# Attention inside a hybrid decoder block: q's and k's split parts made for two heads at once and copied into place, and v's shifted rows loaded into the value tile

## The chip, the cores and the metric

The kernel runs on one core of one Trainium2 chip. The metric is the device time of one execution in microseconds (us); what is given is the median of several runs. One execution was also recorded by the hardware profiler, and all rows of the profile come from it.

The engines carry short names: PE is TensorE (matrix products; PEld is its weight load), DVE is VectorE, ACT is ScalarE, POOL is GpSimd, SP is SyncE, which here issues nearly all DMA transfers. Each engine works through its own queue of instructions in order. L852 is line 852 of the kernel.

## The reference

One layer of a decoder: parallel token mixing (stick-breaking attention with 16 heads of 64, a state-space mixer and two gates), cross-attention into 256 memory tokens, and a gated feed-forward part, each between two norms. The sequence has 1024 tokens, the model 1024 channels, in float32. The change touches the stick-breaking attention only:

```python
z = jnp.einsum('bhtd,bhsd->bhts', qf[:, :, t0:t1], kf[:, :, :t1])   # qf is q / sqrt(64)
causal = jnp.arange(t1)[None, :] < (t0 + jnp.arange(SB_BLOCK))[:, None]
log_1mb = jnp.where(causal, jax.nn.log_sigmoid(-z), 0.0)
tail = lax.cumsum(log_1mb, axis=3, reverse=True)
w = jnp.where(causal, jnp.exp(z + tail), 0.0)
outs.append(jnp.einsum('bhts,bhsd->bhtd', w, vf[:, :, :t1]))
```

A weight is the chance of breaking the stick at position s times the chance of not having broken it between s and t. With N(s) the product of (1 - sigmoid) from s to t, the weight is N(s+1) - N(s), so the sum over s of weight times v can be written with N and with differences of neighbouring rows of v.

## The kernel before

All products are done on PE with each float32 operand split into a high part that PE's format holds and the low rest: hi x hi, hi x lo and lo x hi are added up in PSUM (`mm3`, L101). So every operand needs two instructions on its way: a copy that rounds (mostly on ACT) and a subtraction that gives the rest (mostly on DVE).

The kernel has these stages: projections with the two-level scheme `winograd_pair`, the attention, the state-space mixer, cross-attention and the feed-forward part. The attention is the loop over `m` from L927: a unit is one head and one half (512) of its queries, four units are a pair of heads. While one unit's values are formed, the scores of the next unit and pieces of a projection are interleaved with it (`interleave`, L903).

For each unit:
- `scores` (L837): for each block of 128 queries, two matmuls per 512 keys (L849, L850) with q's tile `qs` as the weights and `kh`, `kl` as the moving operand; ACT takes the sigmoid of the negative (L851), and DVE runs a product scan backwards over the row (L852). The head has 64 channels and PE has 128 rows, so the rows 0 to 63 of `qs` hold the high part of q and the rows 64 to 127 the low part; `kh` holds k's high part in both halves of its rows, `kl` the low part in both. One matmul then gives two of the products.
- `values` (L859): PE transposes the scanned blocks (L868), ACT makes the high part of N - 1 (`wth`, L871), DVE the low part (`wtl`, L872), and two matmuls add them to the head's output with the value tile `v` as the weights (L880, L881). The output's two halves of rows are added by ACT and DVE (L888, L889) and go to memory as `oT`.
- `differences` (L822): for an even head, v's rows and the rows shifted by one are loaded for both heads (`va`, `vb`, L828, one buffer each), POOL subtracts them (L829), and for each head POOL writes the high and low part into the value tile `v` (L833, L834; two buffers, one per head of the pair).

The projections of q and k for a pair of heads are run two pairs ahead (`qk_proj`, L782; `qk_quanta`, L911): `dense` (L758) loads 128 columns of the weights, splits them into `whi` and `wlo`, and forms each half of the result (128 rows, 64 per head) by 24 matmuls into one of two PSUM buffers. When a half is done, it is evacuated: `ev_q` (L786) or `ev_k` (L797). For each head a copy over its 64 rows goes to ACT and a subtraction over 64 rows to DVE; for k, two DMAs then copy rows 0 to 63 of `kh` and `kl` to rows 64 to 127 (L808, L809). `qs`, `kh` and `kl` have four buffers, so those of two pairs.

The order of each engine's instructions is not the program's order: the framework simulates the program with priced instructions, takes what is ready by priority, and lays that order down, with semaphores for what depends on another engine. `issue_behind` (L212) ties a projection's matmuls behind the eighth last marked attention matmul (L772). A tile's buffer is reused only when all that reads the tile before it is done.

Of the kernel before, what the change touches and what calls it, by code (L numbers as in the profile page):

```python
# [16 lines left out]
P = 128  # L17
# [3 lines left out]
NCH = S // P  # L21
HALF = 512
# [3 lines left out]
NH, HD = 16, 64  # L26
# [9 lines left out]
def hybrid_block(ctx, tc, a, out, dbg=None):  # L36
    nc = tc.nc
    V, A, G, T = nc.vector, nc.scalar, nc.gpsimd, nc.tensor

    def pool(stack, name, bufs=1, space=None, side=None):  # L40
        kw = {} if space is None else {"space": space}
        if side is not None:
            kw["side"] = side
        if space is not DRAM:
            kw["reuse_waits"] = "tile"
        return stack.enter_context(tc.tile_pool(name=name, bufs=bufs, **kw))
# [40 lines left out]
    def hi_sb(o, i, eng=None):  # L87
        if eng is None:
            turn[0] += 1
            eng = "pa"[turn[0] % 2]  # L90
        if eng == "p":
            G.tensor_scalar(o, i, 1.0, 0.0, ALU.mult, ALU.add)  # L92
        elif eng == "v":
            V.tensor_copy(o, i)
        else:
            A.activation(o, i, AF.Copy)  # L96

    def lo_of(o, i, hi, eng=V):
        eng.tensor_tensor(o, i, hi.bitcast(F32), ALU.subtract)  # L99
# [151 lines left out]
    with ExitStack() as pa:  # L251
# [382 lines left out]
        with ExitStack() as p1:  # L634
# [4 lines left out]
            t2 = pool(p1, "t2c", 2)  # L639
# [96 lines left out]
        with ExitStack() as p2:  # L736
            wp = pool(p2, "w2", 2, side="right")
            vp = pool(p2, "vp", 2, side="right")
            t2 = pool(p2, "t2b", 2, side="right")
# [18 lines left out]
            def dense(c0, evac):  # L758

                st = {}  # L760

                def first():
                    st["w"] = load_split(wp, colblock(w_in, c0), [P, KT, P], 1)

                def part(half, kk):
                    def run():
                        if kk == 0:
                            st["ps"] = mk(psm, [P, HALF], F32, "mm")
                        whi, wlo = st["w"]
# [12 lines left out]
            def qk_proj(hp):  # L782
                for j in range(2):
                    heads[2 * hp + j] = {}

                def ev_q(ps, half):  # L786
                    sl = slice(half * HALF, (half + 1) * HALF)
                    for j in range(2):
                        hd = heads[2 * hp + j]
                        if half == 0:  # L790
                            hd["q"] = mk(qk, [P, S], F32R, "qs")
                        pj = ps[j * HD:(j + 1) * HD]
                        q = hd["q"]
                        A.activation(q[0:HD, sl], pj, AF.Copy)
                        V.tensor_tensor(q[HD:P, sl], pj, q[0:HD, sl].bitcast(F32), ALU.subtract)

                def ev_k(ps, half):  # L797
                    sl = slice(half * HALF, (half + 1) * HALF)
                    for j in range(2):
                        hd = heads[2 * hp + j]  # L800
                        if half == 0:
                            hd["kh"] = mk(qk, [P, S], F32R, "kh")
                            hd["kl"] = mk(qk, [P, S], F32R, "kl")
                        pj = ps[j * HD:(j + 1) * HD]
                        kh, kl = hd["kh"], hd["kl"]
                        A.activation(kh[0:HD, sl], pj, AF.Copy)
                        V.tensor_tensor(kl[0:HD, sl], pj, kh[0:HD, sl].bitcast(F32), ALU.subtract)
                        nc.sync.dma_start(kh[HD:P, sl].bitcast(F32), kh[0:HD, sl].bitcast(F32))  # L808
                        nc.sync.dma_start(kl[HD:P, sl].bitcast(F32), kl[0:HD, sl].bitcast(F32))  # L809

                return dense(C_Q + hp * P, ev_q), dense(C_K + hp * P, ev_k)

# [9 lines left out]
            def differences(h):  # L822

                j = h % 2
                if j == 0:
                    va, vb = [mk(vp, [P, NCH, P], F32, n, bufs=1) for n in ("va", "vb")]
                    for t, r in ((va, 0), (vb, 1)):
                        nc.sync.dma_start(t, v_d[r:S + r, h * HD:(h + 2) * HD].rearrange("(c p) d -> p c d", p=P))  # L828
                    G.tensor_tensor(va, va, vb, ALU.subtract)  # L829
                    dvs[0] = va  # L830
                dv = dvs[0][:, :, j * HD:(j + 1) * HD]
                vt = mk(vp, [P, NCH, P], F32R, "v")
                hi_sb(vt[:, :, 0:HD], dv, "p")  # L833
                lo_of(vt[:, :, HD:P], dv, vt[:, :, 0:HD], G)  # L834
                heads[h]["v"] = vt
# [91 lines left out]
            for m in range(NM):  # L927
                h, half = m // 2, m % 2
                hp, r = m // 4, m % 4
# [4 lines left out]
                if m >= NM - 5:  # L934
                    n = -(-len(late) // (NM - m))
# [10 lines left out]
    with ExitStack() as p3:  # L946
# [4 lines left out]
        t2 = pool(p3, "s2p", 9)  # L951
# [4 lines left out]
        ps = pool(p3, "ps3", 1, PSUM)  # L956
# [347 lines left out]
    with ExitStack() as p4:  # L1304
# [3 lines left out]
        t2 = pool(p4, "t2m", 4)  # L1308
        ps = pool(p4, "ps4", 4, PSUM)
# [20 lines left out]
        for f in range(KT):  # L1330
# [3 lines left out]
            for half in range(2):  # L1334
                sl = slice(half * HALF, (half + 1) * HALF)
# [77 lines left out]
    with ExitStack() as q1:  # L1413
# [19 lines left out]
    with ExitStack() as q2:  # L1433
# [68 lines left out]
        for m in range(2):  # L1502
            t = mk(t4, [P, D], F32, "x4")
# [36 lines left out]
    with ExitStack() as q4:  # L1540
# [3 lines left out]
        t2 = pool(q4, "t2f", 6, side="right")  # L1544
# [333 lines left out]
```

## Time and profile before

| | |
|---|---|
| Median of 3 runs | 2579.89 us (2579.11 to 2581.29) |
| Profiled execution: time, and span of the records | 2581.7 us, 2580.0 us |
| Attention: first score matmul, last value matmul | 668.3 us, 1091.1 us |
| Distance at which a pair of heads repeats | 49.66 us |
| Granted PE clock between 660 and 1080 us | 1.00 |
| SP issues for k's copies (L808 and L809) | 32 and 32, 128 KB each |

The profile page gives for each engine its busy time and share of the span. Other views of the same execution are used: a table of windows (busy time of every engine in each stretch, granted clock, share of the DMA engines, GB/s), a list of waits (which line of which engine stood for which other, in total, times and longest), and the timeline (start, length, engine, line, output and inputs; in square brackets the idle time of the engine before it and what ended it). Lengths given as three numbers are minimum, median and maximum in ns.

### The profile page before, as it was taken

What the parts mean: (1) busy time and instruction counts of PE and PEld (TensorE: products, weight loads), DVE (VectorE), ACT (ScalarE), POOL (GpSimd) and SP (SyncE); (2) the same over time, 40 slices, a digit from 0 to 9 for tenths busy, and PEclk for the clock granted to TensorE, in tenths of its full rate; (3) what the DMA queues carried; (4) which work ended last, traced back from release to release, by engine and by line L of the source; (5) the groups of instructions that cost most, each with busy time, mean ns of one, the idle gap of its engine ahead of it and who ended that gap; (6) DMA issues with size and microseconds to landing.
All of it is one profiled execution on the core that took longest, in us unless ns stands there. A gap on an engine that the chain in (4) does not pass through costs nothing.

```text
span 2580.0 us, 32652 instructions
## 1 busy us (share of the span) xinstructions
PE 2488.6 (96%) x12026; PEld 2061.7 (80%) x12026; DVE 1819.7 (71%) x2119; ACT 1148.6 (45%) x2052; POOL 882.8 (34%) x690
## 2 busy tenths in 40 slices
PE   8999999999999999979999999999999999999998
PEld 6788787887788788767888788887787888887776
DVE  7685777766688898677888554416459666666997
ACT  6343455555466665556545312314333333334433
POOL 5331554443121121135655231101114323323675
PEclk9999999999999999989999999999999999999999
DMA  6441443334322322355332452311232232234322
GB/s 230 148 154 61 131 135 98 100 108 129 98 78 58 89 69 68 98 164 184 115 92 72 154 165 94 129 51 49 88 113 73 78 96 76 79 95 170 131 98 98
DMA packets 244331, 278.54 MB, mean 108 GB/s; under 512 B 15039, under 2 KB 171848, under 8 KB 243786
## 3 DMA queue, kind: packets, MB, share of 16 engines
q1 hardware_dynamic: 244170, 276.45, 33.7%
q8 instruction: 95, 1.56, 0.2%
q14 instruction: 66, 0.54, 0.1%
HBM read 197.87 MB, written 70.13 MB: 104 GB/s over the span
## 4 chain that ended last, share of the span: by engine, by line
PE 73%; DVE 12%; DMA 6%; issue 4%; ACT 3%; POOL 2%; SPq 0%; POOLq 0%; DVEq 0%; ACTq 0%
PE mm L220 8%; PE mm L222 8%; PE mm L221 8%; PE mm L102 7%; PE mm L104 7%; PE mm L103 7%; PE tr L868 2%; PE p L102 2%; PE p L103 2%; PE p L104 2%; DVE op L99 2%; PE pd L1090 2%; DVE n L852 2%; PE av L881 1%; PE ma L294 1%
## 5 line engine op out<-in xcount | busy, mean ns | idle before, releaser
L852 DVE TENSOR_TENSOR_SCAN n<-n,mask 128x128 f32<-128x128 f32 (+7 forms) x128 | 176.4, 1403 | 11.0 <-ACT n L851 10.3
L99 DVE TENSOR_TENSOR sw<-sf,sw 128x512 fp32r<-128x512 f32 x150 | 129.1, 873 | 66.2 <-ACT sw L96 65.7
L196 POOL TENSOR_TENSOR sf<-wr,wr 128x512 f32<-128x512 f32 x38 | 59.1, 1555 | 287.2 <-DMA wr<-in_w_gu_dram 138.7
L871 ACT ACTIVATE wth<-tr,mone 128x512 fp32r<-128x512 f32 x192 | 110.9, 580 | 73.3 <-PE tr L868 71.7
L96 ACT ACTIVATE sw<-sf 128x512 fp32r<-128x512 f32 x150 | 91.8, 626 | 99.2 <-PE mm L222 84.5
L99 DVE TENSOR_TENSOR sw<-wr,sw 128x512 fp32r<-128x512 f32 x113 | 110.3, 979 | 32.8 <-ACT sw L96 32.8
L872 DVE SCALAR_TENSOR_TENSOR wtl<-tr,wth 128x512 fp32r<-128x512 f32 x192 | 101.6, 546 | 39.9 <-ACT wth L871 38.5
L222 PE MATMUL mm<-h,sw 128*128 128x512 f32 x320 | 124.8, 391 | 1.8 <-DVE sw L99 1.8
L96 ACT ACTIVATE sw<-wr 128x512 fp32r<-128x512 f32 x113 | 70.8, 629 | 124.1 <-PE mm L222 123.9
L220 PE MATMUL mm<-h,sw 128*128 128x512 f32 x320 | 122.6, 391 | 3.1 <-ACT h L96 2.3
L221 PE MATMUL mm<-h,sw 128*128 128x512 f32 x320 | 125.1, 391 | 0.0
L102 PE MATMUL mm<-oth,bw 128*128 128x512 f32 (+1 forms) x320 | 122.4, 382 | 2.5 <-DVE a L1149 2.2
L104 PE MATMUL mm<-oth,bw 128*128 128x512 f32 (+1 forms) x320 | 119.5, 373 | 0.8 <-DVE bw L1136 0.5
L103 PE MATMUL mm<-otl,bw 128*128 128x512 f32 (+1 forms) x320 | 118.9, 371 | 0.0
L92 POOL TENSOR_SCALAR v<-va 128x512 fp32r<-128x512 f32 x16 | 21.0, 1316 | 272.5 <-PE av L881 147.9
L667 DVE SCALAR_TENSOR_TENSOR b<-b,prmT,b 128x1023 f32<-128x1023 f32 (+2 forms) x72 | 106.5, 1481 | 9.9 <-ACT b L665 9.4
L851 ACT ACTIVATE n<-sc 128x512 f32<-128x512 f32 (+1 forms) x192 | 89.0, 486 | 50.4 <-PE sc L850 26.5
L165 POOL TENSOR_SCALAR rstd<-ms 128x1 f32<-128x1 f32 x82 | 27.7, 338 | 239.4 <-ACT x L1370 102.5
L102 PE MATMUL p<-bw,h 128*128 128x512 f32 x256 | 99.5, 394 | 3.3 <-DVE x L1372 2.4
L104 PE MATMUL p<-bw,h 128*128 128x512 f32 x256 | 100.6, 394 | 0.0
L103 PE MATMUL p<-bw,h 128*128 128x512 f32 x256 | 100.5, 393 | 0.0
L198 POOL TENSOR_TENSOR sf<-wr 128x512 f32<-128x512 f32 x38 | 63.2, 1663 | 108.2 <-DVE sw L99 108.2
(592 smaller groups left out, 8171.5 us busy)
## 6 DMA issues: line engine op xcount, KB each, us to landing
wr<-in_w_gu_dram SPq DMA_DIRECT2D x80, 256.0 KB
wr<-in_w_in_dram SPq DMA_DIRECT2D x36, 512.0 KB
zr<-in_w_in_dram SPq DMA_DIRECT2D x32, 512.0 KB
gu_d<-t SPq DMA_DIRECT2D x44, 256.0 KB
wraw<-in_w_in_dram SPq DMA_DIRECT2D x20, 512.0 KB
xs_d<-b SPq DMA_DIRECT2D x32, 256.0 KB
s<-xs_d SPq DMA_DIRECT2D x32, 256.0 KB
s<-zs_d SPq DMA_DIRECT2D x32, 256.0 KB
```

The costliest lines, as they stand in the source:

```text
L96: A.activation(o, i, AF.Copy)
L99: eng.tensor_tensor(o, i, hi.bitcast(F32), ALU.subtract)
L102: first = T.matmul(ps, sh, mh, start=start, stop=False)
L103: T.matmul(ps, sh, ml, start=False, stop=False)
L104: T.matmul(ps, sl, mh, start=False, stop=stop)
L220: T.matmul(ps, w[0][:, k, :], b[0][:, k, :], start=first and k == 0, stop=False, skip_group_check=True)
L221: T.matmul(ps, w[0][:, k, :], b[1][:, k, :], start=False, stop=False, skip_group_check=True)
L222: T.matmul(ps, w[1][:, k, :], b[0][:, k, :], start=False, stop=last and k == 3, skip_group_check=True)
L667: V.scalar_tensor_tensor(acc[:, sh:], y[:, :S - sh], cw(3 - sh, f), acc[:, sh:], ALU.mult, ALU.add)
L852: V.tensor_tensor_scan(nt[:, 0:L][:, ::-1], nt[:, 0:L][:, ::-1], mask[:, S - L:][:, ::-1], 1.0, ALU.mult, ALU.max)
L871: A.activation(wh[:, t0 * P:], pt[:, t0 * P:], AF.Identity, bias=mone)
L872: V.scalar_tensor_tensor(wl[:, t0 * P:], pt[:, t0 * P:], -1.0, wh[:, t0 * P:].bitcast(F32), ALU.add, ALU.subtract)
```

## The change

From the second pair of heads on (`hp > 0`), the evacuation first makes the high and the low part of all 128 rows, of both heads, in two new tiles `hT` and `lT` (one buffer each, in the pool `t2`): one instruction on ACT, one on DVE. DMAs issued by SP then copy 64 rows each to where they belong: for q four per half (two heads, two parts), for k eight per half (two heads, two parts, both halves of the tile's rows). The first pair is evacuated as before. For v, the tile `vb` is gone: the shifted rows are loaded into the even head's value tile `v`, read from there by the subtraction and then overwritten by the head's high and low parts. `vb` took 4 KB of each partition, `hT` and `lT` take 2 KB each.

```diff
+                def split(ps):
+                    hi, lo = [mk(t2, [P, HALF], F32R, n, bufs=1) for n in ("hT", "lT")]
+                    A.activation(hi, ps, AF.Copy)
+                    V.tensor_tensor(lo, ps, hi.bitcast(F32), ALU.subtract)
+                    return hi.bitcast(F32), lo.bitcast(F32)
+
                 def ev_q(ps, half):
                     sl = slice(half * HALF, (half + 1) * HALF)
+                    if hp > 0:
+                        parts = split(ps)
                     for j in range(2):
...
-                        pj = ps[j * HD:(j + 1) * HD]
                         q = hd["q"]
-                        A.activation(q[0:HD, sl], pj, AF.Copy)
-                        V.tensor_tensor(q[HD:P, sl], pj, q[0:HD, sl].bitcast(F32), ALU.subtract)
+                        rows_ = slice(j * HD, (j + 1) * HD)
+                        if hp > 0:
+                            for r, t in enumerate(parts):
+                                nc.sync.dma_start(q[r * HD:(r + 1) * HD, sl].bitcast(F32), t[rows_])
+                        else:
+                            A.activation(q[0:HD, sl], ps[rows_], AF.Copy)
+                            V.tensor_tensor(q[HD:P, sl], ps[rows_], q[0:HD, sl].bitcast(F32), ALU.subtract)
...
                 def ev_k(ps, half):
...
-                        A.activation(kh[0:HD, sl], pj, AF.Copy)
-                        V.tensor_tensor(kl[0:HD, sl], pj, kh[0:HD, sl].bitcast(F32), ALU.subtract)
-                        nc.sync.dma_start(kh[HD:P, sl].bitcast(F32), kh[0:HD, sl].bitcast(F32))
-                        nc.sync.dma_start(kl[HD:P, sl].bitcast(F32), kl[0:HD, sl].bitcast(F32))
+                        if hp > 0:
+                            for d, t in zip((kh, kl), parts):
+                                for r in range(2):
+                                    nc.sync.dma_start(d[r * HD:(r + 1) * HD, sl].bitcast(F32), t[rows_])
+                        else:
...
             def differences(h):

                 j = h % 2
+                vt = mk(vp, [P, NCH, P], F32R, "v")
                 if j == 0:
-                    va, vb = [mk(vp, [P, NCH, P], F32, n, bufs=1) for n in ("va", "vb")]
+                    va, vb = mk(vp, [P, NCH, P], F32, "va", bufs=1), vt.bitcast(F32)
                     for t, r in ((va, 0), (vb, 1)):
                         nc.sync.dma_start(t, v_d[r:S + r, h * HD:(h + 2) * HD].rearrange("(c p) d -> p c d", p=P))
                     G.tensor_tensor(va, va, vb, ALU.subtract)
                     dvs[0] = va
                 dv = dvs[0][:, :, j * HD:(j + 1) * HD]
-                vt = mk(vp, [P, NCH, P], F32R, "v")
```

More of the change, by code (lines that the diff above doesn't have):

```diff
@@ L791, in ev_q @@
                             hd["q"] = mk(qk, [P, S], F32R, "qs")
-                        pj = ps[j * HD:(j + 1) * HD]
                         q = hd["q"]
-                        A.activation(q[0:HD, sl], pj, AF.Copy)
-                        V.tensor_tensor(q[HD:P, sl], pj, q[0:HD, sl].bitcast(F32), ALU.subtract)
+                        rows_ = slice(j * HD, (j + 1) * HD)
[5 more added lines that the diff above has]
+                            V.tensor_tensor(q[HD:P, sl], ps[rows_], q[0:HD, sl].bitcast(F32), ALU.subtract)
                 def ev_k(ps, half):
                     sl = slice(half * HALF, (half + 1) * HALF)
+                    if hp > 0:
+                        parts = split(ps)
                     for j in range(2):
@@ L803, in ev_k @@
                             hd["kl"] = mk(qk, [P, S], F32R, "kl")
-                        pj = ps[j * HD:(j + 1) * HD]
                         kh, kl = hd["kh"], hd["kl"]
-                        A.activation(kh[0:HD, sl], pj, AF.Copy)
-                        V.tensor_tensor(kl[0:HD, sl], pj, kh[0:HD, sl].bitcast(F32), ALU.subtract)
-                        nc.sync.dma_start(kh[HD:P, sl].bitcast(F32), kh[0:HD, sl].bitcast(F32))
-                        nc.sync.dma_start(kl[HD:P, sl].bitcast(F32), kl[0:HD, sl].bitcast(F32))
+                        rows_ = slice(j * HD, (j + 1) * HD)
+                        if hp > 0:
+                            for d, t in zip((kh, kl), parts):
+                                for r in range(2):
+                                    nc.sync.dma_start(d[r * HD:(r + 1) * HD, sl].bitcast(F32), t[rows_])
+                        else:
+                            A.activation(kh[0:HD, sl], ps[rows_], AF.Copy)
+                            V.tensor_tensor(kl[0:HD, sl], ps[rows_], kh[0:HD, sl].bitcast(F32), ALU.subtract)
+                            for t in (kh, kl):
+                                nc.sync.dma_start(t[HD:P, sl].bitcast(F32), t[0:HD, sl].bitcast(F32))
                 return dense(C_Q + hp * P, ev_q), dense(C_K + hp * P, ev_k)
```

## The prediction

> **What bounds the kernel now.** The page comes first: over the whole span TensorE (PE) is busy 96% of the time and VectorE (DVE) 71%. The change touches only the attention stage, so the next view is the table of windows, cut at one head pair (49.66 us, the distance at which the same instruction returns, below).
>
> ```profile
> PE 2488.6 (96%) x12026; PEld 2061.7 (80%) x12026; DVE 1819.7 (71%) x2119; ACT 1148.6 (45%) x2052; POOL 882.8 (34%) x690
> ...
> 713.53:763.19 49.66, 48.21 (x266) 40.36 (x265) 43.84 (x55) 31.39 (x62) 9.74 (x7) 1.00 0.27 75
> 763.19:812.85 49.66, 48.22 (x266) 40.32 (x265) 43.84 (x55) 31.36 (x62) 9.53 (x7) 1.00 0.27 75
> ...
> 961.83:1011.49 49.66, 49.44 (x272) 41.49 (x272) 42.83 (x54) 30.47 (x60) 9.65 (x6) 1.00 0.24 64
> ```
>
> The columns after the length are busy time (instructions) of PE, PEld, DVE, ACT and POOL, the granted clock, the DMA share and GB/s. In a steady pair PE works 48.2 of 49.66 us: 1.45 us idle, all that a faster helper engine can win per pair. DVE works 43.84 us (88%), the next tightest; ACT and POOL are far below. The list of waits of the stage and the two places where PE stands say what ends those idle times:
>
> ```profile
> PE av L881 <- DVE wtl L872: 9.9, 13, 1.2
> PE mm L102 <- DVE qs L795: 1.3, 1, 1.3
> PE tr L868 <- DVE wtl L872: 1.1, 1, 1.1
> ...
> 696.61 0.66 PE L868 MATMUL tr<-ident,n 128*128 128x128 f32 x4 [1.10 <-DVE wtl L872]
> 708.46 0.39 PE L881 MATMUL av<-wtl,v 128*128 128x256 f32 x1 [1.21 <-DVE wtl L872]
> 733.83 0.39 PE L881 MATMUL av<-wtl,v 128*128 128x256 f32 x1 [0.22 <-DVE wtl L872]
> 758.12 0.39 PE L881 MATMUL av<-wtl,v 128*128 128x256 f32 x1 [1.23 <-DVE wtl L872]
> ...
> 1036.51 0.39 PE L881 MATMUL av<-wtl,v 128*128 128x256 f32 x1 [1.25 <-DVE wtl L872]
> ```
>
> From 708.46 to 758.12 is the pair of 49.66 us. The 13 waits of 9.9 us are seven long ones (1.2 us) and six short ones (0.22 us). Six of the seven long ones come eight microseconds after a k evacuation; the seventh, at 1036.51, lies behind the last pair's projections. The reader should look at why DVE is late at 758.12:
>
> ```profile
> 749.29 0.69 DVE L872 SCALAR_TENSOR_TENSOR wtl<-tr,wth 128x512 fp32r<-128x512 f32 x1 [1.23 <-ACT wth L871]
> 750.13 0.68 DVE L807 TENSOR_TENSOR kl<-mm,kh 64x512 fp32r<-64x512 f32 x1
> 750.77 1.49 DVE L852 TENSOR_TENSOR_SCAN n<-n,mask 128x640 f32<-128x640 f32 x1
> 752.18 1.13 DVE L872 SCALAR_TENSOR_TENSOR wtl<-tr,wth 128x512 fp32r<-128x512 f32 x2
> 753.34 0.69 DVE L807 TENSOR_TENSOR kl<-mm,kh 64x512 fp32r<-64x512 f32 x1
> 753.96 3.66 DVE L852 TENSOR_TENSOR_SCAN n<-n,mask 128x768 f32<-128x768 f32 x2
> 757.64 0.62 DVE L872 SCALAR_TENSOR_TENSOR wtl<-tr,wth 128x256 fp32r<-128x256 f32 x2
> ```
>
> From 749.29 to 757.64 DVE has no gap. Between the two scans' inputs stand the two k subtractions of 0.68 us, one per head; the part of the weights (wtl) that PE waits for comes last. So PE sets the pace, and DVE's queue takes 1.45 us per pair from it.
>
> **What the change removes.** From pair 1 on, one ACT copy and one DVE subtraction over 128 rows replace two over 64 rows, for q and k and for both halves: seven pairs times four evacuations, 28 ACT and 28 DVE instructions less.
>
> ```profile
> L807 DVE TENSOR_TENSOR kl<-mm,kh x32: 682/688/694, 661.4 to 1016.6; 64x512 fp32r<-64x512 f32 x32
> L1116 DVE TENSOR_TENSOR otl<-ptr,oth x32: 676/684/694, 1147.3 to 1451.0; 128x512 fp32r<-128x512 f32 x32
> L806 ACT ACTIVATE kh<-mm x32: 590/594/597, 660.8 to 1015.5; 64x512 fp32r<-64x512 f32 x32
> L1115 ACT ACTIVATE oth<-ptr x32: 572/581/602, 1146.3 to 1450.4; 128x512 fp32r<-128x512 f32 x32
> ```
>
> Lines 1115 and 1116 are the same two operations on 128 rows: 684 ns where 64 rows take 688, 581 where they take 594. The full tile costs what half of it costs, so 28 x 0.69 = 19.3 us leave DVE and 28 x 0.59 = 16.5 us leave ACT, 2.76 us of DVE in each pair. That is not the gain: only what shortens a PE wait counts.
>
> The k stall: the subtraction of 753.34 goes, and the scan that starts at 753.96 can start at 753.34 if its input is there. The last copy in its way on ACT goes too (752.28, below), so the input comes earlier as well.
>
> ```profile
> 749.51 0.59 ACT L806 ACTIVATE kh<-mm 64x512 fp32r<-64x512 f32 x1 [0.24 <-PE mm L104]
> ...
> 752.28 0.60 ACT L806 ACTIVATE kh<-mm 64x512 fp32r<-64x512 f32 x1
> 752.90 1.35 ACT L851 ACTIVATE n<-sc 128x256 f32<-128x256 f32 x3
> ...
> 762.92 0.59 ACT L806 ACTIVATE kh<-mm 64x512 fp32r<-64x512 f32 x1 [1.63 <-PE mm L104]
> ...
> 728.92 0.69 DVE L795 TENSOR_TENSOR qs<-mm,qs 64x512 fp32r<-64x512 f32 x1
> ```
>
> The gain is 753.96 - 753.34 = 0.62 us, and 1.23 - 0.62 = 0.61 us of the stall stay. Six times: 3.7 us. The subtraction at 750.13 stays as the merged one; it could not be saved, since the new one waits for the same PE result.
>
> The short stall (733.83) has a q subtraction ahead of it in the same manner (728.92); 0.62 is more than its 0.22, so it goes, six times: 1.3 us. The 1.1 us before 696.61 has pair 1's q subtractions ahead: between 0 and 0.69, and since the oT of the first head also stands in that chain, I take half, 0.35. The 1.3 us behind a q subtraction came once; between 0 and 1.3, and I take 0, since what is in one pair of seven isn't caused by what every pair does.
>
> **What it adds.** Each q half now takes four copies from the parts hT and lT into the heads' tiles, and each k half eight instead of four: 12 issues per half in place of four, so 16 more per pair, 112 in all, of 128 KB each. Their price on the issuing queue and until landing:
>
> ```profile
> L808 SPq DMA_DIRECT2D kh<-kh x32: 461/462/1071, 661.4 to 1016.1; - x32
> 1015.51 2.16 DMA kl<-kl
> ...
> 766.63 0.22 PE L849 MATMUL sc<-kh,qs 128*128 128x128 f32 x1
> ...
> 751.00:752.00 1.00, 1.00 (x7) 0.87 (x6) 1.00 (x1) 1.00 (x3) 0.00 (x0) 1.00 0.62 141
> 752.00:753.00 1.00, 1.00 (x7) 0.78 (x6) 1.00 (x3) 0.95 (x3) 0.00 (x0) 1.00 0.56 129
> ```
>
> SP pays 16 x 0.46 = 7.4 us of 49.66. The two copies of 750.12 and 750.84 moved their 256 KB (135 GB/s over two microseconds) with 1.18 engine shares, 0.59 us each; 16 more add 9.4 us to 0.27 x 49.66 = 13.4, a share of 0.46. Neither is near full. What hides the landing: k's half that is evacuated at 749.5 is first read by the short scores of the next head, here from 766.6, ten microseconds after its copies. Without that cover each would cost its 2.16 us, as the one at 1015.51 that sits on the chain.
>
> The first score matmul of each tile has more DMA arrivals to wait for, each an extra semaphore instruction of 51 ns (row below). Three more for each of 28 head halves: between 0 and 4.3 us. The 25 that are there cause no idle entry on PE in a steady pair, so I take 0.
>
> **What it makes wait.** hT and lT have one buffer each, so an evacuation's ACT copy now waits until the copies of the one before have read it. Behind that ACT instruction stand the score sigmoids and wth, and PE waits for wth. Evacuations lie 11 to 14 us apart (749.51 and 762.92 on ACT for k's halves); subtraction, eight issues and landing take 0.69 + 3.7 + 2.16 = 6.6 us. So 4 us or more to spare: priced at 0.
>
> The value tile now receives the shifted rows, so that load waits until the head two before has done its last value matmul; the old vb was refilled as soon as POOL had subtracted.
>
> ```profile
> L849 PEldq EVENT_SEMAPHORE  x25: 51/51/51, 668.2 to 1032.5; - x25
> SPq L828 <- POOL v L99: 100.4, 7, 16.3
> 738.05 0.37 SPq L828 DMA_DIRECT2D va<-v_d  x1
> 742.79 3.39 POOL L829 TENSOR_TENSOR va<-va,vb 128x1024 f32<-128x1024 f32 x1 [4.76 <-DMA va<-v_d]
> 759.94 0.94 POOL L92 TENSOR_SCALAR v<-va 128x512 fp32r<-128x512 f32 x1 [13.77 <-PE tr L868]
> 760.97 1.30 POOL L99 TENSOR_TENSOR v<-va,v 128x512 fp32r<-128x512 f32 x1
> 784.54 1.76 POOL L92 TENSOR_SCALAR v<-va 128x512 fp32r<-128x512 f32 x1 [20.74 <-PE av L881]
> ```
>
> Today POOL splits the even head's values at 759.94, as soon as the tile is free. Now the load starts there: 742.79 - 738.05 = 4.7 us, the subtraction 3.4, the split 2.3: ready at 770.4 instead of 762.3. The matmuls that read it begin when the head between ends, at 784.5: 14 us to spare. The weight split that POOL does next serves the projection 25 us on. Cost 0.
>
> Sum: 3.7 + 1.3 + 0.35 = 5.4 us off the profiled execution, whose span is 2580.0 and whose time is 2581.7; the median of the runs is 2579.9, so 2574.5.
>
> **A rule against this reading.** The Trainium skill (Perfetto Trace Analysis, "Identifying the Most-Contended Engine") holds matmul busy time for a bad measure of TensorE and takes weight-load busy time instead. By it the order turns: PEld has 40.36 us of 49.66 (81%), DVE 88%. Then DVE would set the pace, which is the fourth rival below; the rows of back-to-back matmuls speak against it.
>
> **Rivals.**
>
> First, all waits of PE on DVE in the stage go (9.9 less the 1.25 at 1036.51, then 1.1 and 1.3, is 11.0): 2569. For it: in the last pair (961.83) DVE has one instruction less and PE is busy 49.44 us. Against: that PE had other matmuls to put there.
>
> Second, nothing is won: each engine's order is laid out by a planner that prices the instructions, and with fewer on DVE it may place the scans or the wtl otherwise, so that a stall of the same size stands elsewhere, or the semaphores cost their 4.3 us. 2577 to 2580.
>
> Third, slower: a load that waits stands ahead of the copies on SP, which issues in order. If the shifted rows' load (free at 759.94) is ahead of k's first eight copies (ready from 750.1 on), these go out from 760.3 to 764.0; the last read of hT lands at about 765.2, and the copy on ACT that is ready at 762.92 waits 2.3 us, wth and PE behind it. Six times is 13.8, less 5.4 won: 2588. It decides once SP is held over 13.4 - 6.6 = 6.8 us; va's load holds it up to 16 us today, so the mechanism is there, but the copies are ready nine microseconds earlier and should be ahead.
>
> Fourth, DVE sets the pace and all of its 19.3 us come off: 2561. Against: PE has 1.45 us idle per pair.
>
> **How the numbers follow.** Forecast 0.50, its own range 2571.5 to 2577.5; first rival 0.15, second 0.18, third 0.15, fourth 0.02. A measurement of this kernel can tell about 0.2% (5.2 us) from no change, so the bound lies at 2574.7, close to the forecast. Faster: somewhat over half of the forecast's share, the first and the fourth, 0.46; slower: most of the third, 0.14; the rest same, 0.40. Range 2567 to 2584: past the first rival, and into the third as far as a smaller hold would reach.
>
> **What would show it.** Right: in the new trace the merged subtraction takes 0.69 us; a steady pair takes about 48.8 us; the wait of av for wtl shrinks to 0.6 us and the short one is gone; no ACT wait on a part's copies. Wrong: a wait of ACT before the hT copy, an idle PE behind a score matmul that waits for DMA, a POOL split later than the head before it ends, or a pair still of 49.7 us with its stall at another place.

## The result, and the profile after

The changed kernel takes 2590.38 us (median of 8 runs, 2586.97 to 2593.05). The runs of the kernel before beside it on the same chip have a median of 2583.01 (8 runs, 2579.11 to 2591.68). The ratio is 1.0024, 95% interval [1.0013, 1.0035]: slower by some 6 us, where 5.4 us less were forecast. The profiled execution took 2590.81 us with a span of 2589.1. The three runs that the prediction started from (2579.89) lie at the low end of what the kernel before does: over the 119 runs that stood beside the experiments it goes from 2577.0 to 2591.7, median 2584.4. So every verdict here is a ratio to runs of the kernel before on the same chip; 0.1% of the time is 2.6 us.

Three pairs in the table of windows of the kernel after (length, then busy time and instructions of PE, PEld, DVE, ACT and POOL, granted clock, DMA share, GB/s):

```profile
756.80:808.00 51.20, 49.21 (x266) 40.58 (x265) 43.40 (x51) 28.35 (x57) 10.13 (x6) 1.00 0.45 114
808.00:859.07 51.07, 49.15 (x266) 40.60 (x265) 43.29 (x51) 28.36 (x57) 10.14 (x6) 1.00 0.45 114
859.07:910.19 51.12, 49.13 (x266) 40.58 (x265) 43.35 (x51) 28.36 (x57) 10.14 (x6) 1.00 0.44 113
```

A pair takes 51.1 us in place of 49.66. DVE has four instructions less, 2.76 us of work, and yet is busy 43.4 us where it was busy 43.84: its other instructions have become longer. Where that is, the timeline shows around the release of the even head's value tile, first POOL, then DVE (start, length, engine, line, operation, output and inputs; in brackets the idle time before and what ended it):

```profile
760.97 2.40 POOL L849 TENSOR_TENSOR va<-va,v 128x1024 f32<-128x1024 f32 x1 [25.75 <-DMA v<-v_d]
763.34 1.69 POOL L92 TENSOR_SCALAR whi<-wraw 128x1024 fp32r<-128x1024 f32 x1
765.00 0.61 POOL L92 TENSOR_SCALAR v<-va 128x512 fp32r<-128x512 f32 x1
765.70 2.11 POOL L99 TENSOR_TENSOR v<-va,v 128x512 fp32r<-128x512 f32 x1
```

```profile
760.53 0.69 DVE L789 TENSOR_TENSOR lT<-mm,hT 128x512 fp32r<-128x512 f32 x1 [0.78 <-ACT hT L788]
761.36 2.83 DVE L871 TENSOR_TENSOR_SCAN n<-n,mask 128x384 f32<-128x384 f32 x1
764.11 0.39 DVE L891 SCALAR_TENSOR_TENSOR wtl<-tr,wth 128x256 fp32r<-128x256 f32 x1
765.07 1.62 DVE L99 TENSOR_TENSOR wlo<-wraw,whi 128x1024 fp32r<-128x1024 f32 x1 [0.56 <-POOL whi L92]
766.61 0.28 DVE L891 SCALAR_TENSOR_TENSOR wtl<-tr,wth 128x128 fp32r<-128x128 f32 x1
766.81 2.09 DVE L871 TENSOR_TENSOR_SCAN n<-n,mask 128x512 f32<-128x512 f32 x1
768.82 0.66 DVE L891 SCALAR_TENSOR_TENSOR wtl<-tr,wth 128x512 fp32r<-128x512 f32 x1
```

The reader should read the two fences against each other. POOL has waited 25.75 us for the shifted rows, and then does its four instructions of this half of the pair in one burst. DVE's scan over 384 columns takes 2.83 us and ends only after POOL's subtraction (763.37); the same scan takes 0.93 in the kernel before (row further down). `wlo` stands 0.56 us for POOL's `whi` and then takes 1.62 where it takes 1.23 undisturbed; the scan over 512 columns runs beside POOL's L99 and takes 2.09 where it took 1.21. DVE's instructions that read PSUM keep their lengths (`lT` 0.69 us, `wtl` over 256 columns 0.39). Together 1.90 + 0.56 + 0.39 + 0.88 = 3.7 us of DVE's queue per pair, in a stretch in which it has no other idle time over 0.15 us (760.53 to 771.6).

What reaches PE stands in the waits of its weight loads at the same place:

```profile
764.56 0.19 PEld L900 LDWEIGHTS av<-wtl,v 128*128 128x128 f32 x1 [0.39 <-DVE wtl L891]
766.94 0.19 PEld L900 LDWEIGHTS av<-wtl,v 128*128 128x128 f32 x1 [0.37 <-DVE wtl L891]
769.53 0.42 PEld L887 LDWEIGHTS tr<-ident,n 128*128 128x128 f32 x4 [0.85 <-DVE wtl L891]
770.25 0.19 PEld L899 LDWEIGHTS av<-wth,v 128*128 128x128 f32 x1 [0.30 <-DVE oT L908]
```

That is 1.9 us of waiting in six microseconds. On PE's own line only 0.43 of it is idle time (before 769.53); the rest lies inside what counts as busy, which fits that PE "busy" rose from 48.2 to 49.2 us a pair with the same instructions. In the kernel after the waits of PE from 660 to 1095 us are (total, times, longest):

```profile
PE av L900 <- DVE wtl L891: 7.1, 8, 1.2
PE tr L887 <- DVE wtl L891: 4.0, 9, 0.7
PE av L899 <- DVE oT L908: 3.2, 6, 0.5
```

The attention, from its first score matmul to its last value matmul, takes 430.7 us in place of 422.8, so 7.9 us more. It also starts 2.9 us earlier (665.4 and 668.3), and the rest of the kernel behind it takes 4.1 us longer, which is within what that rest varies by in the runs below (1486.3 to 1496.5 us). So the 9.1 us by which the two profiled spans differ are not all the attention's.

### The profile page after: what moved, and what is told of

Read it like the earlier page. It is cut to its first block, busy times and chain, and to the rows that moved or that the text cites. A ratio compares the mean times of both kernels' runs of the same rounds, so it can differ in the third digit from the quotient of the medians.

```text
span 2589.1 us, 32733 instructions
## 1 busy us (share of the span) xinstructions
PE 2499.5 (97%) x12026; PEld 2068.8 (80%) x12026; DVE 1815.1 (70%) x2091; ACT 1127.6 (44%) x2024; POOL 889.8 (34%) x690
## 5 line engine op out<-in xcount | busy, mean ns | idle before, releaser
L871 DVE TENSOR_TENSOR_SCAN n<-n,mask 128x128 f32<-128x128 f32 (+7 forms) x128 | 191.4, 1516 | 18.7 <-ACT n L870 17.9
L99 DVE TENSOR_TENSOR sw<-sf,sw 128x512 fp32r<-128x512 f32 x150 | 126.8, 858 | 65.2 <-ACT sw L96 64.7
L99 DVE TENSOR_TENSOR sw<-wr,sw 128x512 fp32r<-128x512 f32 x113 | 110.9, 984 | 33.1 <-ACT sw L96 33.1
L220 PE MATMUL mm<-h,sw 128*128 128x512 f32 x320 | 122.6, 391 | 3.1 <-ACT h L96 2.3
L887 PE MATMUL tr<-ident,n 128*128 128x128 f32 x576 | 94.8, 275 | 4.1 <-DVE wtl L891 4.0
```

The lines of the kernel that those rows point to most:

```text
L220: T.matmul(ps, w[0][:, k, :], b[0][:, k, :], start=first and k == 0, stop=False, skip_group_check=True)
L871: V.tensor_tensor_scan(nt[:, 0:L][:, ::-1], nt[:, 0:L][:, ::-1], mask[:, S - L:][:, ::-1], 1.0, ALU.mult, ALU.max)
```

## The experiments

In the table the pair is the mean of five, from POOL's split of an odd head's values (its L92 on v) near 735 us to the one near 985; the attention is measured as above. The other three runs (`before_room`, `before_sub4`, `parts_sub4_psv2`) have their numbers in the text.

| run | v into value tile | subtraction | whi on | pair us | attention us | ratio [95%] |
|---|---|---|---|---|---|---|
| before | no | whole | POOL, ACT | 50.00 | 422.8 | 1 |
| after | yes | whole | POOL, ACT | 51.16 | 430.7 | 1.0024 [1.0013, 1.0035] |
| parts_only | no | whole | POOL, ACT | 49.55 | 420.3 | 0.9974 [0.9965, 0.9983] |
| v_only | yes | whole | POOL, ACT | 51.15 | 432.5 | 1.0028 [1.0018, 1.0037] |
| sub_on_dve | yes | on DVE | POOL, ACT | 51.67 | 432.5 | 1.0017 [1.0007, 1.0027] |
| after_sub4 | yes | 4 pieces | POOL, ACT | 51.49 | 431.7 | 1.0026 [1.0017, 1.0036] |
| after_sub1 | yes | an eighth | POOL, ACT | 52.11 | 435.1 | 1.0038 [1.0025, 1.0050] |
| parts_sub4 | no | 4 pieces | POOL, ACT | 49.53 | 419.0 | 0.9964 [0.9951, 0.9976] |
| after_whi_act | yes | whole | ACT | 50.78 | 427.3 | 1.0043 [1.0026, 1.0060] |
| after_sub1_whi_act | yes | an eighth | ACT | 49.51 | 419.0 | 1.0004 [0.9993, 1.0014] |
| after_sub4_whi_act | yes | 4 pieces | ACT | 49.49 | 418.3 | 1.0008 [0.9997, 1.0020] |
| parts_sub4_whi_act | no | 4 pieces | ACT | 49.50 | 419.9 | 1.0004 [0.9993, 1.0015] |
| after_whi_late | yes | whole | ACT from pair 3 | 50.94 | 428.8 | 1.0012 [1.0002, 1.0021] |
| after_sub4_whi_late | yes | 4 pieces | ACT from pair 3 | 49.54 | 419.8 | 0.9985 [0.9975, 0.9995] |
| parts_sub4_whi_late | no | 4 pieces | ACT from pair 3 | 49.49 | 419.8 | 0.9980 [0.9970, 0.9989] |

"POOL, ACT" means that every second weight tile's high part is made by POOL, the others by ACT. The mean of before holds one disturbed pair (below); the others take 49.66. Two means hold pairs in which PE's clock fell: `after_sub1` (53.2 us in two pairs, 51.05 to 51.66 in the others) and `sub_on_dve` (53.2 in one, 51.2 to 51.4 in the others).

**Which half of the change loses: parts_only, v_only, before_room.** `parts_only` takes the merged parts of the diff and leaves `differences` as it was; `v_only` is the edit of `differences` alone. The parts' room came from two other pools, and `before_room` has only that:

```diff
-    stats = pool(ctx, "stats", 16)
+    stats = pool(ctx, "stats", 8)
-                    gt = mk(t2, [P, HALF], F32, "gt")
+                    gt = mk(t2, [P, HALF], F32, "gt", bufs=1)
```

> The merged parts of q and k alone: the shifted rows keep their own tile vb. The 4 KB for hT and lT come from one buffer of the tile gt instead of two and from 8 instead of 16 buffers of the norm statistics. Theory A (collision: in the changed kernel POOL's subtraction va - v and its splits fall into a stretch in which DVE scans, and DVE stands until POOL is done): here POOL subtracts where it did before, the scan over 384 columns behind the k subtraction takes 0.94 us again instead of 2.7, a pair takes 48.6 to 49.2 us, the ratio to the kernel before is 0.997 to 0.999. Theory B (the parts themselves cost: copies, semaphores, single buffers, another planned order): a pair still takes about 51.1 us, ratio about 1.002 or more.

> The shifted rows loaded into the value tile alone; q's and k's evacuation as before. Theory A: the subtraction falls behind the release of the value tile, DVE stands some 3 us per pair and has no relief: a pair of 51.5 to 53 us, ratio 1.004 to 1.008, slower than the changed kernel. Theory B: a pair of 49.7 us, ratio 1.000.

> The kernel before with only what makes room in the run beside it: one buffer of gt, 8 buffers of the norm statistics. Both theories: no difference, ratio 0.999 to 1.001, a pair of 49.7 us. If it differs by more, the run beside it is read against this one.

Measured: the parts alone are faster (0.9974), v's edit alone slower (1.0028) with the pair of the kernel after, the room changes nothing (1.0005 [0.9994, 1.0017]; attention 423.0). So the loss is v's. Both sizes were off: the pair of `parts_only` (49.55) lies above what theory A gave (48.6 to 49.2), the pair of `v_only` (51.15) and its ratio below (51.5 to 53, 1.004 to 1.008). The windows of one pair of each, `parts_only` first, then `v_only`:

```profile
785.19:834.73 49.54, 48.19 (x266) 40.65 (x265) 40.75 (x51) 28.37 (x58) 9.74 (x6) 1.00 0.45 117
```

```profile
734.18:785.26 51.08, 48.88 (x267) 40.38 (x266) 46.34 (x55) 31.46 (x62) 9.83 (x6) 1.00 0.27 73
```

DVE's busy time says it in one number: 43.84 before, 40.75 with the parts, 46.34 with v's edit, whose instructions on DVE are those of before. The DMA share (0.45 and 0.27) comes with the parts, and the run that has it without v's edit is the faster one.

**The subtraction off POOL: sub_on_dve.**

```diff
-                    G.tensor_tensor(va, va, vb, ALU.subtract)
+                    V.tensor_tensor(va, va, vb, ALU.subtract)
```

> The changed kernel with the subtraction va - v on DVE instead of POOL. Theory A: DVE pays 1.2 us per pair itself but no longer stands 1.8 us for POOL's 2.4 us: a pair of 50 to 50.7 us, ratio to the kernel before 1.000 to 1.0018, below the changed kernel's 1.0024. Theory B: DVE has more to do and nothing else changes: a pair of 51.1 us or more, ratio 1.0024 or above.

Measured: pair 51.67, no gain in the attention: the pair is what theory B gave, the ratio (1.0017) what theory A gave. DVE takes over 1.23 us of work and waits 1.03 us at that place, by the profile for POOL's `whi`, and POOL's L99 still stretches the scan over 384 columns to 2.03. It left open whether the subtraction is the cause at all.

**The subtraction cut or nearly removed: after_sub4, after_sub1.**

```diff
-                    G.tensor_tensor(va, va, vb, ALU.subtract)
+                    for c in range(0, NCH, 2):
+                        G.tensor_tensor(va[:, c:c + 2], va[:, c:c + 2], vb[:, c:c + 2], ALU.subtract)
```

`after_sub1` does only the first of the eight chunks, so it leaves out seven eighths of the differences and its output is not the reference's.

> The kernel after, with POOL's subtraction (2.40 us over 128x1024) cut into four instructions of two chunks each; nothing else. Theory A (DVE stands for the whole of a POOL instruction that reads SBUF): a scan that meets the subtraction now waits for one piece of about 0.6 us in place of 2.4; the scan over 128x384 falls from 2.69 to 1.6 us or less, the long POOL L99 (2.12 us) still stretches what it meets. Of the 1.5 us per pair about 0.9 comes back: pair 50.2 to 50.6 us, ratio to before 0.9995 to 1.0012. Theory C (POOL's subtraction is only late, so something behind the values is late): nothing changes or it gets worse, pair 51.1 or more, ratio 1.0024 or more.

> The kernel after, with POOL's subtraction done on the first of the eight chunks only, so seven eighths of the difference of v's rows are left out (the output is not the reference's); loads, waits and splits of v stay. Theory A: the subtraction's share of the collision goes, DVE's scan over 128x384 is near 0.95 us again unless POOL's split by L99 takes its place; pair 49.9 to 50.5 us, ratio 0.9985 to 1.0010. Theory C (the later load and its waits cost, not the subtraction's length): pair 51.1 us, ratio 1.0020 to 1.0030.

Both missed theory A's range, and on the far side: 51.49 and 52.11 us. Theory A, the stretched scans alone, falls. The timeline of POOL and DVE in `after_sub4` shows why:

```profile
763.24 3.48 POOL L850 TENSOR_TENSOR va<-va,v 128x256 f32<-128x256 f32 x4 [25.48 <-DMA v<-v_d]
...
763.95 1.54 DVE L872 TENSOR_TENSOR_SCAN n<-n,mask 128x384 f32<-128x384 f32 x1
765.41 0.39 DVE L892 SCALAR_TENSOR_TENSOR wtl<-tr,wth 128x256 fp32r<-128x256 f32 x1
767.78 1.62 DVE L99 TENSOR_TENSOR wlo<-wraw,whi 128x1024 fp32r<-128x1024 f32 x1 [1.97 <-POOL whi L92]
...
769.52 2.09 DVE L872 TENSOR_TENSOR_SCAN n<-n,mask 128x512 f32<-128x512 f32 x1
```

The scan fell to 1.54 us as expected, but POOL's pieces now wait for DVE in turn, so the four take 3.48 us in place of 2.40; `whi`, queued behind them on POOL, comes later, and `wlo` waits 1.97 in place of 0.56. What DVE won in the scan it lost in the wait. In `after_sub1` DVE's order puts `wlo` ahead of the scan; DVE, then PE, then one window of a microsecond:

```profile
764.66 1.62 DVE L99 TENSOR_TENSOR wlo<-wraw,whi 128x1024 fp32r<-128x1024 f32 x1 [1.22 <-POOL whi L92]
766.20 2.02 DVE L871 TENSOR_TENSOR_SCAN n<-n,mask 128x384 f32<-128x384 f32 x1
```

```profile
768.59 0.39 PE L900 MATMUL av<-wtl,v 128*128 128x256 f32 x1 [1.84 <-DVE wtl L891]
768.82 0.86 PE L887 MATMUL tr<-ident,n 128*128 128x128 f32 x4
...
926.49 0.39 PE L900 MATMUL av<-wtl,v 128*128 128x256 f32 x1 [1.90 <-DVE wtl L891]
926.71 0.60 PE L887 MATMUL tr<-ident,n 128*128 128x128 f32 x4
```

```profile
769.00:770.00 1.00, 1.00 (x6) 0.90 (x5) 0.87 (x1) 0.29 (x1) 0.00 (x0) 0.51 0.67 125
```

PE's stall grew to 1.84 us, and the granted clock fell to 0.51 behind it (a transpose group of 0.60 us takes 0.86), though not behind the like stall of a later pair. Without the two pairs in which the clock fell `after_sub1` takes 51.05 to 51.66 us a pair, so cutting the subtraction down gave nothing back.

Theory D followed: what costs is not the subtraction but the burst. POOL works in order, and `whi` stands behind the subtraction, which now waits for the tile's release; `wlo` on DVE waits for `whi`, and scans and `wtl` stand behind `wlo`.

**whi off POOL: after_whi_act, after_sub1_whi_act, after_sub4_whi_act, parts_sub4_whi_act.** The high part of all of the attention stage's projection weights goes to ACT, with the subtraction whole, reduced, and cut:

```diff
-                    st["w"] = load_split(wp, colblock(w_in, c0), [P, KT, P], 1)
+                    st["w"] = load_split(wp, colblock(w_in, c0), [P, KT, P], 1, "a")
```

> The kernel after, with the high part of every weight tile of the attention's projections made by ACT (today every second one, 763.34 on POOL, stands behind the subtraction there, and DVE's wlo behind it). Theory D (what costs is the whole burst of POOL that v's later load has moved to the release of the value tile: DVE's wlo waits for POOL's whi, 0.56 us, and runs 0.4 slower, beside the scans that the subtraction and L99 stretch by 1.75 and 0.88): wlo's wait and stretch go, the scans stay stretched; pair 50.2 to 50.8 us, ratio to before 0.9995 to 1.0012. Theory A (the stretched scans alone): pair 51.0 to 51.3, ratio 1.0020 to 1.0030. If ACT's extra 1.06 us delays a wth instead: 51.5 or more.

> As the last, and POOL's subtraction on one chunk of eight only (the differences of the other seven chunks are left out). Only L92 and L99 of v are left in POOL's burst. Theory D: neither the wait of wlo (1.22 us with the subtraction shortened) nor the subtraction's stretch is left, PE's stall of 1.84 us goes and with it the three microseconds at half the clock behind it; pair 49.5 to 50.2 us, ratio 0.997 to 0.9995. Theory C (the loads into the value tile cost by themselves): pair 51 us or more, ratio 1.002 or more.

> The kernel after, with the weights' high part on ACT and POOL's subtraction in four pieces. Theory D: no wait of wlo, and a scan that meets the subtraction waits for one piece of 0.6 to 0.7 us; L99 stretches one scan by 0.9 as before. Pair 49.7 to 50.4 us, ratio 0.998 to 1.0003. If only the lock counted, the pieces would have won on their own already, and this one is no better than they were (1.0026).

> The merged parts alone, the subtraction in four pieces, and the weights' high part on ACT. In this kernel POOL's whi stands 0.71 us behind the release by PE's L103 and nothing waits for it, so theory D expects no change: ratio 0.996 to 0.9972, pair 49.5 us. If moving whi to ACT wins by itself, whatever v does, the ratio is under 0.995.

By the pair, theory D holds: whole 50.78, an eighth 49.51, four pieces 49.49, and the control without v's edit 49.50. With both undone, v's load into the value tile costs nothing in the pair. By the whole kernel all four were over what was expected, the control too (1.0004 for 0.996 to 0.9972), so the extra time belongs to `whi` on ACT and not to v. A part of it lies before the attention. ACT and PE of `parts_sub4_whi_act`, with PE's window behind it:

```profile
629.63 1.06 ACT L96 ACTIVATE whi<-wraw 128x1024 fp32r<-128x1024 f32 x1 [3.72 <-DMA wraw<-in_w_in_dram]
630.60 0.58 ACT L688 ACTIVATE b<-mm 128x512 f32<-128x512 f32 x1
...
633.33 0.80 PE L220 MATMUL mm<-t2h,sw 128*128 128x512 f32 x1 [3.81 <-ACT b L230]
```

```profile
634.00:640.00 6.00, 6.00 (x18) 4.69 (x17) 3.18 (x4) 1.43 (x3) 0.00 (x0) 0.62 0.42 122
```

The same matmul in `parts_sub4`:

```profile
633.35 0.50 PE L220 MATMUL mm<-t2h,sw 128*128 128x512 f32 x1 [1.55 <-ACT b L230]
```

ACT stands 3.72 us for a weight tile of the first pair, copies that PE waits for stand behind it, and the clock falls to 0.62 over six microseconds. All four runs have that wait of PE at 3.2 to 3.8 us; the clock fell behind it in three of them, and not in `after_whi_act`.

**whi on ACT only within the attention: after_whi_late, after_sub4_whi_late, parts_sub4_whi_late.**

```diff
+                eng = "a" if hp >= 2 else None
-                return dense(C_Q + hp * P, ev_q), dense(C_K + hp * P, ev_k)
+                return dense(C_Q + hp * P, ev_q, eng), dense(C_K + hp * P, ev_k, eng)
```

> The kernel after, with the weights' high part on ACT from the third pair's projections on only (hp >= 2, those that are loaded within the attention); the first two pairs' stay as they were, so that ACT doesn't stand for a load at 629.6 to 631.5, before the attention, where the runs with all of them on ACT had PE wait 3.2 to 3.8 us in place of 1.6. Theory D: pair 50.7 us as with all on ACT (the uncut subtraction still stretches a scan), the stretch before the attention as in the kernel after; ratio to before 1.0005 to 1.0020. If the part before the attention wasn't what cost the rest: 1.003 or more.

> As the last, and POOL's subtraction in four pieces: both halves of theory D undone, nothing of v's load or of the parts changed. Pair 49.5 us, attention 418 to 420 us against 422.8 before and 430.7 after, first score matmul at 668 us or earlier; ratio 0.9960 to 0.9980. If the load of v into the value tile costs by itself, or something outside the attention did: 0.999 or more.

> The control of the last without v's part: merged parts, subtraction in pieces, whi on ACT from hp >= 2. Theory D: the pair was 49.5 us with whi on POOL and on ACT, so the ratio is that of the pieces alone, 0.9960 to 0.9975. If ACT's whi costs within the attention: 0.999 or more.

Measured: pairs of 50.94, 49.54 and 49.49 us, ratios 1.0012, 0.9985 and 0.9980. The pairs are within 0.25 us of what was expected, the wait of L220 is 1.6 us again in all three. All three ratios are 0.0023 to 0.0031 below those with all of `whi` on ACT, so the first two pairs' weights made most of the extra time. The second and the third ratio are 0.0005 above their ranges; the one with v's edit and its control agree within their intervals, so what is left over is not v's; what it is wasn't found. The two timelines of DVE side by side show both halves of the cause, `after_whi_late` first:

```profile
761.81 2.40 POOL L850 TENSOR_TENSOR va<-va,v 128x1024 f32<-128x1024 f32 x1 [25.39 <-DMA v<-v_d]
...
761.95 3.34 DVE L99 TENSOR_TENSOR wlo<-wraw,whi 128x1024 fp32r<-128x1024 f32 x1 [1.01 <-ACT whi L96]
```

```profile
761.36 5.43 POOL L851 TENSOR_TENSOR va<-va,v 128x256 f32<-128x256 f32 x4 [25.64 <-DMA v<-v_d]
...
761.26 1.23 DVE L99 TENSOR_TENSOR wlo<-wraw,whi 128x1024 fp32r<-128x1024 f32 x1 [1.03 <-ACT whi L96]
763.00 0.95 DVE L873 TENSOR_TENSOR_SCAN n<-n,mask 128x384 f32<-128x384 f32 x1
```

With the uncut subtraction it is now `wlo` that stands until POOL is done (3.34 us for 1.23). With the pieces the roles turn: POOL stretches to 5.43 us, while DVE's `wlo` and the scan over 384 columns have their own lengths (the scan over 512 still takes 1.58 for 1.21). POOL's lateness costs nothing that shows in the pair, since nothing of DVE waits for it any more. `wlo` still waits a microsecond, now for ACT's `whi`, in both.

**Before's own race: before_sub4, parts_sub4.** In the kernel before, the subtraction and a scan become ready within 0.2 us of each other. In five of the six pairs from 735 us on DVE is first; in the profiled execution's pair from 883.89 to 935.19 (51.30 us) POOL was (and so in `before_room`, where the same pair takes 51.4 us):

```profile
742.77 1.21 DVE L852 TENSOR_TENSOR_SCAN n<-n,mask 128x512 f32<-128x512 f32 x1
...
890.41 0.93 DVE L852 TENSOR_TENSOR_SCAN n<-n,mask 128x384 f32<-128x384 f32 x1
891.59 2.38 POOL L829 TENSOR_TENSOR va<-va,vb 128x1024 f32<-128x1024 f32 x1 [4.55 <-DMA va<-v_d]
891.77 3.28 DVE L852 TENSOR_TENSOR_SCAN n<-n,mask 128x512 f32<-128x512 f32 x1
895.83 0.50 PE L102 MATMUL mm<-t1h,whi 128*128 128x512 f32 x1 [1.32 <-DVE qs L795]
```

That is the wait of 1.3 us behind a q subtraction that "came once", and that the prediction priced at 0 without a cause. Both runs have the subtraction in four pieces, in the kernel before and in `parts_only`.

> The kernel before, with POOL's subtraction in four pieces; nothing else. Theory A with the race (in each pair POOL's subtraction and DVE's scan over 128x512 become ready within 0.2 us; where POOL is first, the scan takes 3.28 us instead of 1.21 and PE stands 1.3 us): a lost race now costs 0.6 us at most, so the runs come together at their low end, 2579 to 2582 us, ratio 0.998 to 0.9995, and no pair of the profiled execution is over 50.2 us. Rival (the spread of before's runs, 2579 to 2591 us, has nothing to do with POOL): median and spread as before's, ratio 0.9995 to 1.0005.

> The merged parts of q and k alone (v loaded as before; gt with one buffer and stats with 8 make room), and POOL's subtraction in four pieces. Theory A: the parts alone already keep POOL's subtraction behind the scan, so pieces win little more: pair 49.4 to 49.6 us, 2575 to 2579 us, ratio 0.9965 to 0.998, and a narrower spread than 2574.4 to 2581.2. Rival (pieces cost POOL's start-up three more times and collide more often): ratio 0.9985 or more.

Measured: `before_sub4` 0.9988 [0.9979, 0.9997], no disturbed pair (mean 49.65 us, attention 421.3), runs from 2578.7 to 2585.9. `parts_sub4` 0.9964 [0.9951, 0.9976], median 2576.6 us, from five runs: the lowest ratio here, though its interval overlaps that of `parts_only`, and faster than both kernels. So a lost race costs time. That it makes the whole spread of the kernel before isn't shown: the range is narrower than on the same chip beside it (2578.9 to 2589.0) but did not collapse, and over the 119 runs the times also go with the mean granted clock (2586.2 us on average at 0.991, 2581.7 at 0.993).

**Where the parts' gain went: parts_sub4_psv2.** In every kernel with merged parts and one `av` buffer PE stands 0.53 us a pair at a place where it did not stand before. Waits of PE in the attention and after it, `parts_sub4`:

```profile
PE av L901 <- DVE wtl L892: 6.0, 7, 1.2
PE av L900 <- DVE oT L909: 3.4, 7, 0.5
```

```diff
-            psc = pool(p2, "psc", 3, PSUM)
+            psc = pool(p2, "psc", 2, PSUM)
-            psv = pool(p2, "psv", 1, PSUM)
+            psv = pool(p2, "psv", 2, PSUM)
```

> Merged parts and pieces, with two PSUM buffers for the head's output av and two instead of three for the scores. In the kernels with merged parts PE stands 0.53 us per pair where the next head's first value matmul waits for oT, which reads the only av buffer; this wait was not there before the change. Theory G (the gain of the merged parts, forecast at 0.84 us per pair, came to 0.13 because the stall moved to oT): without that wait the pair is 48.9 to 49.1 us, ratio 0.9950 to 0.9962. Rival (two score buffers cost more, or the stall moves on to wtl again): pair 49.5 us or more, ratio 0.9964 or more.

Measured: pair 49.03 us, as theory G expected, and attention 416.0, with PE's waits now

```profile
PE tr L888 <- DVE wtl L892: 3.1, 9, 0.5
PE av L900 <- ACT wth L891: 2.7, 1, 2.7
```

The ratio, 0.9976 [0.9965, 0.9988], lies above theory G's range (0.9950 to 0.9962) and does not show the 3 us won: after the attention this profiled execution took 1495.5 us, that of `parts_sub4` 1489.2, and the executions of all these kernels lie between 1486.3 and 1496.5 there. So the gain is shown in the stage and not in the whole time.

## Why the prediction was wrong

**The step that failed** is the moved POOL work. It was priced at "Cost 0" because POOL and PE have room: the split ready at 770.4, the matmuls at 784.5, "the weight split that POOL does next serves the projection 25 us on". The first half held: v's split is done at 767.8, and no matmul waits for it. What was left out is DVE. Its instructions depend on POOL's hour in two ways: scans stretch when they meet POOL's subtraction or its L99, and `wlo` waits for `whi`, because the order laid down puts it into DVE's queue long before the projection needs it. The runs price it at 1.6 us a pair (51.16 with v's edit, 49.55 without it) and 10.4 over the attention (430.7 and 420.3). Neither a shorter subtraction (51.49, 52.11) nor `whi` elsewhere (50.78, 50.94) removes it alone; both together do (49.49 to 49.54, the pair without v's edit). The mechanism stood in the prediction's own row: the subtraction of 742.79 that it priced at 3.39 us takes 2.38 where no scan comes first.

The Trainium skill (SBUF — State Buffer, "Who interferes with whom") has a rule that spoke against the step and was not weighed: a DVE instruction with two inputs in SBUF contends with a GpSimd instruction that reads SBUF, the port pair that they share is an exclusive lock, and the order of issue decides who is blocked. The trace agrees in both directions: scan 2.83 us for 0.93 (after) and `wlo` 3.34 for 1.23 (`after_whi_late`) when POOL is first, the subtraction 3.39 for 2.38 when DVE is (before), and `lT` and `wtl`, which read PSUM, at their usual lengths.

**Held.** The merged instructions cost what half of them did: `lT` 0.69 us, `hT` 0.59. DMA share 0.45 a pair (0.46 forecast), and the waits of the stage name no copy out of hT or lT. ACT stood once before an hT copy for a DMA (3.0 us, by the profile one of the first pair's k copies); the third rival, SP held by a waiting load, did not happen: v's load went out at 756.80, the next k copies at 760.53, when `hT` was just made. Its 2588 us lie near the measured 2590 by chance. The short q stall went. The fourth rival is answered by `parts_only`, where DVE's busy time fell by 3.1 us a pair and the pair by 0.11.

**Mis-sized.** The k stall was to fall from 1.23 to 0.61 us; it fell to 0.81 (`parts_only`). The first pair's stall, taken at 0.35 us off, fell by 0.42, from 1.10 to 0.68. The short stall's 0.22 went, but 0.53 appeared before the next head's first value matmul, on `oT`. So the merged parts gave 49.66 - 49.55 = 0.11 us a pair in place of 0.62 + 0.22 = 0.84. The second rival named this ("a stall of the same size stands elsewhere") and had 0.18. With a second `av` buffer, and one score buffer less, 0.5 us more a pair comes out. That `parts_only` is nevertheless faster by 0.26% has a further reason in the trace: its pairs have none of the lost races of the kernel before, since its scan over 512 columns is first in all six: by 0.65 us at 740.01, by 0.08 to 0.85 in the others. How much of the ratio that makes was not measured apart; the pieces alone, which take the races out of the kernel before, are worth 0.12%.

**The baseline.** The sum went against 2579.9, and the kernel before stands at 2584.4 over all its runs. That shifts the forecast's absolute time by some 4 us and doesn't touch its sign, which was wrong.

## What to carry to other kernels

When work moves to a later point on an engine with room, list what stands behind it in that engine's queue and who waits for each, on the waiter's queue as well as at the last consumer: an instruction that is needed "25 us on" may be waited for at once by another in-order engine. Then look for what runs at the new time on DVE and GpSimd with all inputs in SBUF; if both do, the one that comes later can stand until the other is done (0.93 us became 2.83 here), so cut the one that isn't on the path into pieces, and make sure that nothing waits for those. An engine that does less work and stays as busy is the sign to look for: here DVE, 2.76 us less work a pair and 43.4 us busy for 43.84.

## What the runs showed of the hardware that was not expected

A wait of PE much shorter than 3 us can have some three microseconds at half the clock behind it. In `after_sub1` PE stood 1.3 to 1.9 us in each steady pair. Behind the 1.84 us that end at 768.59 the clock was 0.51 from 769 on and full again by 773; behind the 1.90 us that end at 926.49 it stayed at 1.00 and the transposes kept their usual 0.60 us. The same fall came behind 1.83 us (873.27) there and behind 1.87 us (870.92) in `sub_on_dve`, and behind none of the shorter waits of the two runs' steady pairs (up to 1.75 us). What tells the 1.90 us from the others is open. The Trainium skill (TensorE: Matmul & The Clock Gate, Part 1 on the clock gate) gives an activity window of about 3.4 us that runs freely and puts the fall after at least one idle window. In the 5 us ahead of the fall at 769 PE was busy for 3.16 us and its longest wait was the 1.84, so no such window stood idle; the measured fall decides.

An instruction of POOL cut into pieces costs little as such and much in company: the subtraction in four pieces takes 2.80 us, for 2.38 to 2.40 uncut, where no scan and no `wlo` of DVE runs beside it (748.18 in `parts_sub4_whi_act`), and 5.43 us where both do (761.36 in `after_sub4_whi_late`).
